# Second block's mixer: three projection blocks split with GpSimd, the convolution's sums in PSUM

## The chip, the cores and the metric

One core of one Trainium2 chip runs the program. The metric is the device time of one execution in microseconds (us). The median of three runs of the kernel before is 1846.14 us (1843.38 to 1847.57).

## What is computed

Two transformer blocks run one after the other on 256 tokens of width 1024, all in float32. The first (two layers, the second with eight experts) is not touched. The second block begins with a mixer, and the change lies there. Cut to what matters:

```python
u = rms_norm(h, mix_norm_g)
q, k, v, glu_a, glu_g = split(u @ w_in)              # 5 x 512 columns
attn_out = moba_attention(q, k, v, rel_bias)         # 8 heads
x = glu_a * sigmoid(glu_g)
x = causal_conv(x, conv_w, 31 taps, per channel) + conv_b
conv_out = silu(layer_norm(x))
h = h + concat(attn_out, conv_out) @ w_out
u = rms_norm(h, ffn_norm_g)
h = h + (silu(u @ w_gate) * (u @ w_up)) @ w_down
```

## The kernel before

**Weights.** All weight matrices come as blocks of 128 x 2048 floats (1 MB). `Stream` (line 52) loads them in a fixed order through SyncE's DMA queue into three raw buffers (`wraw`, `_load`, line 79) and makes two fp32r parts of each (`_split`, line 91): `wh`, a rounded copy made on ScalarE (line 102), and `wl`, the rest, raw minus `wh`, made on VectorE (line 103). A product is then three passes on TensorE, high by high, high by low, low by high (`mm3`). There are three pairs of buffers for the parts, and a fourth during the output products. A raw buffer is free again when `wl` has been made, a pair when the products that read it are done.

A block in `native` is not split: it is multiplied as plain float32 from its raw buffer against an unsplit copy of the input (`xTf`), which TensorE runs as two records for each product (64 for two blocks of 16 products). Its raw buffer is free when these products are done.

**The mixer.** The ten blocks of `w_in_2` are numbered 0 to 9 here: 0 to 3 give gate and value of the four channel tiles of the convolution, 4 and 5 give q, 6 and 7 k, 8 and 9 v. `NATIVE2` says which are native: 0, 1, 4, 5, 6, 7. Blocks 2 and 3, and v's 8 and 9, are split. After each of the blocks 0 to 3 ScalarE makes the sigmoid `ga` (line 1215) and VectorE the product `ug` (line 1216).

`conv(ct)` (line 1226) works on one tile of 128 channels by 256 tokens: ScalarE starts the sum with the last tap and the bias (line 1228), and VectorE adds 30 taps, each one `scalar_tensor_tensor` with a shift of `back` columns, in place in the SBUF tile `cv` (line 1232). The loop behind it issues, for each of four steps, `conv(i)`, the attention scores of two pairs of heads, for the first two steps a block of v, and the values of the step before. Then come the mean over channels (`pmu`, two groups of products on TensorE), the variance (`pvr`), the root on GpSimd, `prs`, SiLU on ScalarE, the split of the result into `oT`, and the output products `Mix.part` into the accumulators `acc0` (PSUM banks 0 and 1, first half of the tokens) and `acc1` (banks 2 and 3). `acc` holds the two halves of 512 output columns in one bank each.

The framework sorts the instructions of each engine by the order in the program and by its estimate of when each is ready, so operations of `conv(1)` can stand between those of `conv(0)`. Each engine then runs its list in order, and waits on semaphores for other engines. Before the change GpSimd has nothing to do from 1535.7 us to 1622.3 us.

Of the kernel before, what the change touches and what calls it, by code (L numbers as in the profile page):

```python
# [10 lines left out]
F32 = mybir.dt.float32  # L11
# [4 lines left out]
AF = mybir.ActivationFunctionType  # L16
ALU = mybir.AluOpType
# [4 lines left out]
T = 256  # L22
# [5 lines left out]
NE = 8  # L28
R_RAW = 3
N_SPLIT = 3  # L30
NATIVE2 = (0, 1, 4, 5, 6, 7)


class Buffers:


    def __init__(self):
        self.pools = []
# [14 lines left out]
class Stream:  # L53

    def __init__(self, tc, raw_pool, pool, blocks, n_raw=R_RAW, n_split=N_SPLIT, native=()):
        self.tc, self.nc = tc, tc.nc
        self.blocks, self.native = blocks, native
        self.raw_bufs, self.split_bufs = Buffers(), Buffers()  # L60
        self.raw_bufs.add(raw_pool, "wraw", n_raw, len(blocks))
        self.split_bufs.add(pool, None, n_split, len(blocks))
        self.ready, self.raws = [], []
        self.n_raw = self.n_used = 0
        self.first = False
        self.limit = len(blocks)
        self.after = ()
        self.load_after = None
        self.before = {}
# [22 lines left out]
    def _split(self, pool):  # L92
        nc = self.nc
        raw = self.raws.pop(0)
        i = self.n_used + len(self.ready)
        wh = pool.tile([P, 2048], F32R, tag="wh", name="wh")
        wl = pool.tile([P, 2048], F32R, tag="wl", name="wl")
        with ExitStack() as queued:
            for ins in self.after:
                queued.enter_context(self.tc.issue_after(ins.ins))  # L100
            for c in self._parts(i):
                nc.scalar.activation(wh[:, c], raw[:, c], AF.Copy)  # L102
                nc.vector.tensor_tensor(wl[:, c], raw[:, c], wh[:, c].bitcast(F32), op=ALU.subtract)  # L103
        self.ready.append((wh, wl))

    def resume(self, after=(), n=None):
# [36 lines left out]
def tile_model(ctx, tc, io, out):  # L143
    nc = tc.nc
    cp = ctx.enter_context(tc.tile_pool(name="cp", bufs=1))
    xp = ctx.enter_context(tc.tile_pool(name="xp", bufs=6))
    rawp = ctx.enter_context(tc.tile_pool(name="rawp", bufs=R_RAW))
    wp = ctx.enter_context(tc.tile_pool(name="wp", bufs=N_SPLIT))
# [3 lines left out]
    def ffn_order(w1, w3, w2, n, lag=1):  # L152
        r = []
        for j in range(n):
            r += [w1[j], w3[j]]
            if j >= lag:
                r.append(w2[j - lag])
        return r + [w2[j] for j in range(n - lag, n)]

    NF, NM = FF // 256, FFE // 512  # L160
    order = [io["w_ab"][i] for i in range(15)] + [io["w_out_ab"][i] for i in range(4)]
# [5 lines left out]
    for i in range(len(steps_) + 1):  # L167
        if i < len(steps_):
            e, j = steps_[i]
            moe_order += [io[n][e][j][kh] for n in ("w1_m", "w3_m") for kh in range(2)]  # L170
        if i:
            e, j = steps_[i - 1]
# [3 lines left out]
    second = len(order)  # L176
    order += [io["w_in2"][i] for i in range(10)] + [io["w_out2"][i] for i in range(4)]
    order += ffn_order(io["w1_2"], io["w3_2"], io["w2_2"], NF)
    ws = Stream(tc, rawp, wp, order, native=[second + i for i in NATIVE2])

    groups = {"acc": (0, 1, 2, 3), "mm": (4, 5, 6, 7), "lg4": (0, 1, 2, 3), "lg": (2, 3), "ppt": (4, 5), "po": (6,),
              "pj": (7,), "acc0": (0, 1), "acc1": (2, 3)}
# [2 lines left out]
    def bank(group, name):  # L185

        i = groups[group][turns[group] % len(groups[group])]
        turns[group] += 1
        return ps.tile([P, 512], F32, tag="bank%d" % i, name=name)
# [19 lines left out]
    def half(nh):  # L209
        return slice(nh * 512, (nh + 1) * 512)  # L210
# [8 lines left out]
    def load_const(pool, name):  # L219
        ap = io[name]  # L220
        t = pool.tile(list(ap.shape), F32, tag=name, name=name, bufs=1)
        load_small(t, ap)
        return t
# [276 lines left out]
    class Mix:  # L500


        def __init__(self, oT, finish):
            self.oT, self.finish = oT, finish
            self.w, self.acc = [], [None, None]
# [49 lines left out]
    with tc.tile_pool(name="l0", bufs=1) as lp:  # L555
# [9 lines left out]
        with tc.tile_pool(name="gla", bufs=1) as gp:  # L565
# [22 lines left out]
            for i in range(2):  # L588
                o = proj_cols(xT)
# [11 lines left out]
            for tt in range(2):  # L601
# [3 lines left out]
                for q in range(2):  # L605
# [5 lines left out]
                    for j in range(2):  # L611
                        rl = g2([P, 2, 256], "rl")
                        nc.scalar.activation(rl[:, :, :S], pis[j][:, :, :S], AF.Relu)
                        for i in range(2):
# [3 lines left out]
                                                           op0=ALU.mult, op1=ALU.add)  # L618
                            first = False
                for r in range(8):  # L620
# [4 lines left out]
                                               op0=ALU.not_equal, op1=ALU.max)  # L625
# [76 lines left out]
            for tt in range(2):  # L702
# [13 lines left out]
                for h in range(4):  # L716
                    nc.vector.scalar_tensor_tensor(o_s[:, h, :], o_s[:, h, :], rs[:, h:h + 1], sg[:, tt, tok(h)],
                                                   op0=ALU.mult, op1=ALU.mult)
# [246 lines left out]
    with tc.tile_pool(name="moer", bufs=4) as mr, tc.tile_pool(name="moe2", bufs=2) as m2:  # L965
# [209 lines left out]
        with tc.high_priority():  # L1175
            for tt in range(2):
# [4 lines left out]
                for nh in range(2):  # L1181
                    c = half(nh)
# [3 lines left out]
                for nh in range(2):  # L1186
                    c = half(nh)
# [9 lines left out]
    with tc.tile_pool(name="s1", bufs=1) as lp:  # L1197
# [3 lines left out]
        cw = load_const(lp, "conv_w")  # L1201
        cpar = load_const(lp, "conv_p")
# [6 lines left out]
        ug = lp.tile([P, 4, T], F32, tag="ug", name="ug")  # L1209
        ga = lp.tile([P, 4, T], F32, tag="ga", name="ga")  # L1210
        cv = lp.tile([P, 4, T], F32, tag="cv", name="cv")
        ws.first = True
        for ct in range(4):
            o = proj_cols(xT, xTf)
# [8 lines left out]
        v = lp.tile([P, 2, 512], F32, tag="v", name="v")  # L1223
        scores, values = attention(t2, t2, qT, kT, v, lambda h: strip[:, h, :], None, oT, 0, on_act=True)

        def conv(ct):

            nc.scalar.activation(cv[:, ct, :], ug[:, ct, :], AF.Identity, bias=cpar[:, 0, ct:ct + 1],
                                 scale=cw[:, ct, 30:31])
            for j in range(30):  # L1230
                back = 30 - j
                nc.vector.scalar_tensor_tensor(cv[:, ct, back:], ug[:, ct, :T - back], cw[:, ct, j:j + 1],  # L1232
                                               cv[:, ct, back:], op0=ALU.mult, op1=ALU.add)

        for i, step in enumerate(STEPS):
            conv(i)
# [5 lines left out]
        with tc.tile_pool(name="t2", bufs=1) as tp, tc.tile_pool(name="t2w", bufs=1) as wo:  # L1242
# [35 lines left out]
            for ct in range(4):  # L1278
                nc.scalar.activation(cv[:, ct, :], cv[:, ct, :], AF.Silu, bias=cpar[:, 2, ct:ct + 1],
                                     scale=cpar[:, 1, ct:ct + 1])  # L1280
# [6 lines left out]
    with tc.tile_pool(name="f2", bufs=2) as fp, tc.tile_pool(name="f2r", bufs=4) as fr, tc.tile_pool(name="f2w", bufs=1) as fw:  # L1287
        fing = bcast(fp, io["fin_g"], "fing")

        o = xp.tile([P, 2, D], F32, tag="b8", name="o")  # L1290
# [149 lines left out]
```

## Time and profile before

| | |
|---|---|
| median of three runs | 1846.14 us |
| the profiled execution: its time / its span | 1845.33 / 1843.5 us |
| TensorE products busy, whole span | 1782.0 us (97%) |
| VectorE busy | 1338.1 us (73%) |
| ScalarE busy | 1096.1 us (59%) |
| GpSimd busy | 83.9 us (5%) |
| mean granted TensorE clock | 0.98 |

In the rows below PE is TensorE, PEld its weight loads, DVE VectorE, ACT ScalarE, POOL GpSimd, SPq SyncE's queue. A row of a timeline gives the start in us from the span's start, the busy time, engine, line, operation, output and inputs, shapes and count; a bracket says how long the engine sat idle before and what ended that. A row that stands for several operations (x14) is a run of them with nothing between. Durations of neighbours on one engine overlap a little, so the step from one start to the next is shorter than the duration. L195 is the line of a helper that issues all products.

### The profile page before, as it was taken

The numbers are of one execution on the slowest core, as the hardware profiler recorded it, in microseconds if no ns is written. First come the engines' busy times: TensorE is split into PE (matmuls) and PEld (weight loads), VectorE is DVE, ScalarE is ACT, GpSimd is POOL, SyncE is SP. The second block draws the span as 40 slices with busy tenths as digits, with TensorE's granted clock in tenths as the row PEclk, the third lists the DMA queues.
The fourth block names the chain that finished last, engine by engine and source line by source line (L and its number), as shares of the span: only waits on it lengthen the run. The fifth ranks groups of instructions, "written<-read, shape, count | busy, mean of one in ns | idle before, by whom it ended". The sixth has DMA issues, their size and how long they took to land. (4 is left out here: it accounts for less than half of the span.)

```text
span 1843.5 us, 24483 instructions
## 1 busy us (share of the span) xinstructions
PE 1782.0 (97%) x9857; PEld 1512.4 (82%) x9857; DVE 1338.1 (73%) x1363; ACT 1096.1 (59%) x1016; POOL 83.9 (5%) x133
## 2 busy tenths in 40 slices
PE   8999999999999999999999999999998987999998
PEld 7887999888778888888788787887886867889997
DVE  6866544545678888888888888888887877955443
ACT  5454433344567777777777777777775754564442
POOL 1101100010010000000000000000002002000000
PEclk9999999999989999999999999999999998999999
DMA  8442985254379999999999999999998933546530
GB/s 297 161 163 103 390 329 186 89 196 158 117 300 423 381 371 371 382 355 366 374 367 368 381 364 375 371 368 373 366 364 321 361 139 140 206 155 250 190 125 24
DMA packets 75418, 512.50 MB, mean 278 GB/s; under 512 B 8572, under 2 KB 8725, under 8 KB 17312
## 3 DMA queue, kind: packets, MB, share of 16 engines
q1 hardware_dynamic: 66096, 475.62, 68.2%
q0 software_dynamic: 8912, 34.70, 5.0%
q8 instruction: 80, 1.31, 0.3%
q10 hardware_dynamic: 288, 0.52, 0.1%
q14 instruction: 42, 0.34, 0.0%
HBM read 495.57 MB, written 19.96 MB: 280 GB/s over the span
## 5 line engine op out<-in xcount | busy, mean ns | idle before, releaser
L103 DVE TENSOR_TENSOR wl<-wraw,wh 128x2048 fp32r<-128x2048 f32 (+1 forms) x446 | 1011.3, 2284 | 306.6 <-ACT wh L102 304.8
L102 ACT ACTIVATE wh<-wraw 128x2048 fp32r<-128x2048 f32 (+1 forms) x446 | 851.8, 1912 | 465.5 <-issue 133.3
L195 PE MATMUL hh<-wl,eTh 128*128 128x512 f32 x896 | 356.0, 397 | 5.2 <-DVE wl L103 5.2
L195 PE MATMUL hh<-wh,eTh 128*128 128x512 f32 x896 | 355.6, 397 | 0.0
L195 PE MATMUL hh<-wh,eTl 128*128 128x512 f32 x896 | 353.5, 395 | 0.0
L195 PE MATMUL pc<-xTh,wh 128*128 128x256 f32 x944 | 270.8, 287 | 1.0 <-ACT xTh L203 1.0
L195 PE MATMUL pc<-xTl,wh 128*128 128x256 f32 x944 | 269.7, 286 | 0.8 <-DVE xTl L204 0.8
L195 PE MATMUL pc<-xTh,wl 128*128 128x256 f32 x944 | 269.6, 286 | 0.0
L195 PEld LDWEIGHTS hh<-wl,eTh 128*128 128x128 f32 x896 | 169.3, 189 | 47.8 <-DVE wl L103 9.5
L195 PEld LDWEIGHTS hh<-wh,eTh 128*128 128x128 f32 x896 | 169.1, 189 | 38.9 <-ACT eTh L203 0.2
L195 PEld LDWEIGHTS hh<-wh,eTl 128*128 128x128 f32 x896 | 169.0, 189 | 38.2
L195 PE MATMUL acc<-wl,mah 128*128 128x512 f32 x448 | 181.7, 406 | 5.9 <-DVE wl L103 5.9
L195 PEld LDWEIGHTS pc<-xTh,wh 128*128 128x128 f32 x944 | 183.2, 194 | 4.0 <-ACT xTh L203 1.4
L195 PEld LDWEIGHTS pc<-xTl,wh 128*128 128x128 f32 x944 | 183.1, 194 | 2.0 <-DVE xTl L204 1.3
L195 PEld LDWEIGHTS pc<-xTh,wl 128*128 128x128 f32 x944 | 183.3, 194 | 0.2 <-issue 0.2
L195 PE MATMUL acc<-wh,mal 128*128 128x512 f32 x448 | 177.6, 397 | 0.3 <-DVE mal L204 0.3
L195 PE MATMUL acc<-wh,mah 128*128 128x512 f32 x448 | 164.2, 396 | 0.5 <-ACT mah L203 0.5
L195 PEld LDWEIGHTS acc<-wl,mah 128*128 128x128 f32 x448 | 85.0, 190 | 24.2 <-DVE wl L103 6.4
L195 PEld LDWEIGHTS acc<-wh,mah 128*128 128x128 f32 x448 | 84.7, 189 | 20.7 <-ACT mah L203 0.9
L195 PEld LDWEIGHTS acc<-wh,mal 128*128 128x128 f32 x448 | 85.2, 190 | 18.5 <-DVE mal L204 0.8
L195 PE MATMUL pt<-wh,xTh 128*128 128x256 f32 x256 | 74.2, 291 | 0.5 <-ACT xTh L203 0.4
L195 PE MATMUL pt<-wl,xTh 128*128 128x256 f32 x256 | 73.6, 288 | 0.2 <-DVE wl L103 0.2
(332 smaller groups left out, 1851.8 us busy)
## 6 DMA issues: line engine op xcount, KB each, us to landing
wraw<-in_w_m_dram SPq DMA_DIRECT2D x336, 1024.0 KB, 7.3
wraw<-in_w_d_dram SPq DMA_DIRECT2D x33, 1024.0 KB, 5.7
wraw<-in_w_dram SPq DMA_DIRECT2D x33, 1024.0 KB, 4.9
wraw<-in_w_ab_dram SPq DMA_DIRECT2D x14, 1024.0 KB, 4.9
wraw<-in_w_cd_dram SPq DMA_DIRECT2D x12, 1024.0 KB, 4.9
wraw<-in_w_in_dram SPq DMA_DIRECT2D x10, 1024.0 KB, 4.9
xg_d<-zero POOLq DMA_DIRECT2D x8, 1024.0 KB, 43.8
rows<-scr POOLq DMA_DIRECT2D x3, 1536.0 KB, 11.6
```

The source lines that it names most:

```text
L102: nc.scalar.activation(wh[:, c], raw[:, c], AF.Copy)
L103: nc.vector.tensor_tensor(wl[:, c], raw[:, c], wh[:, c].bitcast(F32), op=ALU.subtract)
L195: nc.tensor.matmul(o, l, r, start=start, stop=stop, skip_group_check=True)
```

## The change

Block 5 stays native beside 0 and 1; blocks 4, 6 and 7 are now split, their high parts on ScalarE as for all blocks, their low parts on GpSimd. The convolution's running sums move from the SBUF tile `cv` to two PSUM banks, `sums`, tiles 0 and 1 in the first and 2 and 3 in the second, which take the turns of `acc0`. The last tap of each tile writes `cv`; it does not reach column 0, which ScalarE copies.

```diff
--- before.py
+++ after.py
@@ -28,7 +28,8 @@
 NE = 8
 R_RAW = 3
 N_SPLIT = 3
-NATIVE2 = (0, 1, 4, 5, 6, 7)
+NATIVE2 = (0, 1, 5)
+POOL2 = (4, 6, 7)
 
 
 class Buffers:
@@ -54,9 +55,9 @@
 
 
 
-    def __init__(self, tc, raw_pool, pool, blocks, n_raw=R_RAW, n_split=N_SPLIT, native=()):
+    def __init__(self, tc, raw_pool, pool, blocks, n_raw=R_RAW, n_split=N_SPLIT, native=(), on_pool=()):
         self.tc, self.nc = tc, tc.nc
-        self.blocks, self.native = blocks, native
+        self.blocks, self.native, self.on_pool = blocks, native, on_pool
         self.raw_bufs, self.split_bufs = Buffers(), Buffers()
         self.raw_bufs.add(raw_pool, "wraw", n_raw, len(blocks))
         self.split_bufs.add(pool, None, n_split, len(blocks))
@@ -100,7 +101,8 @@
                 queued.enter_context(self.tc.issue_after(ins.ins))
             for c in self._parts(i):
                 nc.scalar.activation(wh[:, c], raw[:, c], AF.Copy)
-                nc.vector.tensor_tensor(wl[:, c], raw[:, c], wh[:, c].bitcast(F32), op=ALU.subtract)
+                engine = nc.gpsimd if i in self.on_pool else nc.vector
+                engine.tensor_tensor(wl[:, c], raw[:, c], wh[:, c].bitcast(F32), op=ALU.subtract)
         self.ready.append((wh, wl))
 
     def resume(self, after=(), n=None):
@@ -176,7 +178,8 @@
     second = len(order)
     order += [io["w_in2"][i] for i in range(10)] + [io["w_out2"][i] for i in range(4)]
     order += ffn_order(io["w1_2"], io["w3_2"], io["w2_2"], NF)
-    ws = Stream(tc, rawp, wp, order, native=[second + i for i in NATIVE2])
+    ws = Stream(tc, rawp, wp, order, native=[second + i for i in NATIVE2],
+                on_pool=[second + i for i in POOL2])
 
     groups = {"acc": (0, 1, 2, 3), "mm": (4, 5, 6, 7), "lg4": (0, 1, 2, 3), "lg": (2, 3), "ppt": (4, 5), "po": (6,),
               "pj": (7,), "acc0": (0, 1), "acc1": (2, 3)}
@@ -1223,14 +1226,19 @@
         v = lp.tile([P, 2, 512], F32, tag="v", name="v")
         scores, values = attention(t2, t2, qT, kT, v, lambda h: strip[:, h, :], None, oT, 0, on_act=True)
 
+        sums = [bank("acc0", "cv") for _ in range(2)]
+
         def conv(ct):
 
-            nc.scalar.activation(cv[:, ct, :], ug[:, ct, :], AF.Identity, bias=cpar[:, 0, ct:ct + 1],
-                                 scale=cw[:, ct, 30:31])
+
+            o = sums[ct // 2][:, ct % 2 * T:(ct % 2 + 1) * T]
+            nc.scalar.activation(o, ug[:, ct, :], AF.Identity, bias=cpar[:, 0, ct:ct + 1], scale=cw[:, ct, 30:31])
             for j in range(30):
                 back = 30 - j
-                nc.vector.scalar_tensor_tensor(cv[:, ct, back:], ug[:, ct, :T - back], cw[:, ct, j:j + 1],
-                                               cv[:, ct, back:], op0=ALU.mult, op1=ALU.add)
+                last = j == 29
+                nc.vector.scalar_tensor_tensor((cv[:, ct] if last else o)[:, back:], ug[:, ct, :T - back], cw[:, ct, j:j + 1],
+                                               o[:, back:], op0=ALU.mult, op1=ALU.add)
+            nc.scalar.activation(cv[:, ct, 0:1], o[:, 0:1], AF.Copy)
 
         for i, step in enumerate(STEPS):
             conv(i)
```

## Rows read from the trace of the kernel before

**Rows 1.** Busy time by stage: start and end, length, engines, granted clock, DMA.
```profile
1545.20:1616.10 70.90, 67.89 (x418) 60.21 (x418) 69.34 (x176) 32.96 (x66) 0.00 (x0) 0.98 0.53 186
1616.10:1644.80 28.70, 28.43 (x160) 22.57 (x159) 14.97 (x23) 19.18 (x37) 1.84 (x5) 1.00 0.23 84
```
**Rows 2.** Timeline of VectorE, the convolution's taps.
```profile
1545.24 2.92 DVE L1232 SCALAR_TENSOR_TENSOR cv<-ug,conv_w,cv 128x226 f32<-128x226 f32 x6 [0.67 <-ACT cv L1228]
...
1550.61 5.41 DVE L1232 SCALAR_TENSOR_TENSOR cv<-ug,conv_w,cv 128x232 f32<-128x232 f32 x14
...
1561.90 20.97 DVE L1232 SCALAR_TENSOR_TENSOR cv<-ug,conv_w,cv 128x247 f32<-128x247 f32 x55
...
1606.50 3.04 DVE L1232 SCALAR_TENSOR_TENSOR cv<-ug,conv_w,cv 128x247 f32<-128x247 f32 x6
...
1615.08 0.48 DVE L1232 SCALAR_TENSOR_TENSOR cv<-ug,conv_w,cv 128x255 f32<-128x255 f32 x1
```
**Rows 3.** Groups by line: count, busy us, mean ns, idle; wl 1545-1615.5, wh 1505-1650.
```profile
L103 DVE TENSOR_TENSOR wl<-wraw,wh 128x2048 fp32r<-128x2048 f32 x7 | 15.9, 2282 | 0.9 <-ACT wh L102 0.9
...
L102 ACT ACTIVATE wh<-wraw 128x2048 fp32r<-128x2048 f32 x13 | 24.8, 1911 | 14.4 <-DMA wraw<-in_w_in_dram 8.8 <-PE acc L195 3.4 <-PE pt L195 1.3
```
**Rows 4.** Timeline of TensorE, the projection blocks.
```profile
1534.70 14.58 PE L195 MATMUL pc<-xTf,wraw 128*128 128x256 f32 x64
1548.92 0.47 PE L195 MATMUL pc<-xTh,wh 128*128 128x256 f32 x1
...
1560.62 27.79 PE L195 MATMUL pc<-xTf,wraw 128*128 128x256 f32 x128
1588.34 0.72 PE L195 MATMUL lg<-kT,qT 64*128 64x128 f32 x8
```
**Rows 5.** Timeline of all engines around the end of block 2.
```profile
1551.86 0.28 PE L195 MATMUL pc<-xTh,wl 128*128 128x256 f32 x1
...
1554.74 0.28 PE L195 MATMUL pc<-xTh,wl 128*128 128x256 f32 x1
...
1555.06 0.39 ACT L1215 ACTIVATE ga<-pc 128x256 f32<-128x256 f32 x1 [3.73 <-PE pc L195]
...
1555.93 0.41 DVE L1216 TENSOR_TENSOR ug<-ga,pc 128x256 f32<-128x256 f32 x1
...
1556.27 1.22 DVE L1232 SCALAR_TENSOR_TENSOR cv<-ug,conv_w,cv 128x240 f32<-128x240 f32 x3
...
1556.38 0.60 ACT L1228 ACTIVATE cv<-ug,conv_p,conv_w 128x256 f32<-128x256 f32 x1 [0.94 <-DVE ug L1216]
```
**Rows 6.** Timeline of GpSimd and VectorE in the first block, around 75 us.
```profile
75.08 3.97 POOL L646 TENSOR_TENSOR sg<-sg,gnorm 128x1024 f32<-128x1024 f32 x1 [26.65 <-ACT sg L644]
...
74.54 2.29 DVE L103 TENSOR_TENSOR wl<-wraw,wh 128x2048 fp32r<-128x2048 f32 x1 [3.46 <-ACT wh L102]
77.91 1.28 DVE L668 TENSOR_TENSOR QK<-E,kaT 128x128 f32<-128x128 f32 x1 [1.08 <-ACT E L663]
...
79.32 0.28 DVE L668 TENSOR_TENSOR QK<-E,kaT 128x128 f32<-128x128 f32 x1
```
**Rows 7.** Issues by line: count, KB each, median us from issue to landing.
```profile
wraw<-in_w_in_dram SPq DMA_DIRECT2D x10, 1024.0 KB, 4.9
```
**Rows 8.** Groups of VectorE by line, inputs in PSUM (po) and in SBUF (cv).
```profile
L204 DVE TENSOR_TENSOR oTl<-po,oTh 128x256 fp32r<-128x256 f32 x4 | 1.7, 417 | 2.4 <-ACT oTh L203 2.3
...
L204 DVE TENSOR_TENSOR oTl<-cv,oTh 128x256 fp32r<-128x256 f32 x4 | 1.5, 418 | 0.0
```
**Rows 9.** Timelines of ScalarE, TensorE and VectorE from 1612 to 1636 us.
```profile
1617.99 1.06 ACT L1261 ACTIVATE ga<-cv 128x1024 f32<-128x1024 f32 x1 [0.74 <-DVE cv L1260]
...
1612.21 0.58 PE L195 MATMUL acc<-wh,oTh 128*128 128x512 f32 x1
...
1620.16 1.84 PE L195 MATMUL pvr<-c,ga 128*128 128x1 f32 x16
...
1634.50 0.62 PE L195 MATMUL acc<-wh,oTl 128*128 128x512 f32 x2
...
1633.82 1.09 DVE L204 TENSOR_TENSOR oTl<-cv,oTh 128x256 fp32r<-128x256 f32 x3
```
**Rows 10.** Timeline of TensorE, the stall ahead of v's second block.
```profile
1600.51 0.77 PE L481 MATMUL ppt<-ident,z 128*128 128x128 f32 x2 [1.27 <-ACT z L470]
```

## Prediction

> **What bounds the kernel now.** The page comes first: TensorE is busy almost throughout, but that is a mean over stages, so I go to the stage that the change edits, the second block's mixer, from the first projection product at 1534.70 us to the last output product at about 1644.8. The table by stage cuts it at the end of the convolution [rows 1]. In the 70.90 us up to 1616.10 VectorE is busy 69.34 and TensorE 67.89; in the 28.70 us behind it TensorE is busy 28.43 and VectorE 14.97. So two engines take turns: VectorE sets when the convolution ends, TensorE fills the rest. What VectorE does in that first stretch is read from its timeline and its groups [rows 2, 3]: the convolution is 120 operations of L1232 (4 channel tiles by 30 taps), between them 7 low parts wl at 2.28 us, and the softmax pieces. The first tap starts at 1545.24 and the last ends at 1615.47. Nothing in the change makes the start earlier: the first two blocks, on which it waits, stay native.
>
> **Part 1: three blocks leave plain float32.** Four native blocks stand back to back from 1560.62 to 1588.34, 27.72 us, so 6.93 each; the two split ones before them fill 1548.92 to 1560.62, 5.85 each [rows 4]. Each of blocks 4, 6, 7 saves 1.08 us on TensorE, 3.2 us in all: the projections would end at 1585.1.
>
> **Part 2: their high and low parts.** ScalarE gets three more high parts at 1.91 us [rows 3]. They fall between 1549 and 1567, where ScalarE sits idle between gates (3.73 us before the one at 1555.06 [rows 5]), so I cost them at nothing; if that cover were gone, 5.7 us of ScalarE stand ahead of the gates. GpSimd makes the low parts. Its price is in the first block: a 128x1024 product of two SBUF tensors lasts 3.97 us from 75.08, but it starts under a VectorE low part that began at 74.54 and ends at 76.83. Counted from there to 79.05 it is 2.22 us, so 4.4 for 2048 (an estimate from this row; 7.9 if all of the 3.97 were its own) [rows 6]. Then by block: a load lands in 4.9 us [rows 7], the high part takes 1.9, the low part 4.4 to 7.9. Block 4's raw buffer comes free at about 1541.8, when block 0's products end (half of the 14.2 us of [rows 4]), so its low part is there by 1553 to 1557, wanted at 1560.6. Block 6 loads behind block 3's low part (1550.4): ready by 1562 to 1565.1 plus any sharing of the transfer, wanted at 1573.4. Block 7 loads into the buffer that GpSimd's own subtract releases: ready by 1566 to 1573, wanted at 1579.2. Even the slow ends leave 3 us. SyncE's queue is passed in order: the loads of blocks 7, 8, 9 now wait for GpSimd's subtracts instead of products that end 10 us later, so a late subtract would hold all later loads; on time, it brings them forward. GpSimd's next work is the root after the variance, at 1622, long after.
>
> That same place shows the price of GpSimd and VectorE reading SBUF together: an L668 of two SBUF tensors, normally 0.28 us, took 1.28, ending with GpSimd's 79.05 [rows 6]. [...] The low parts wl still have two; by my times none of them meets a GpSimd subtract (block 3's runs 1548 to 1550.4, block 8's after 1570), so I add nothing, and up to 4.4 us for each that does.
>
> **Part 3: the sums in PSUM.** Removed is nothing; 120 taps remain, the last of each tile writing SBUF, and four one-column copies come on ScalarE. What a tap costs when it reads and writes PSUM no row shows. The nearest: the low part of an attention output read from PSUM lasts 417 ns, that of a convolution output read from SBUF 418 [rows 8]. Reading PSUM costs nothing; writing is not shown. Ends: below, the 0.34 us step of a plain 256-column operation against 0.38 of a tap, if PSUM shed the difference, −4.8 us over 120; above, +0.11 us each, what a tap alone pays (next paragraph), +13 us. I take 0, by the reading rows.
>
> [...]
>
> **The order it forces.** A tap on the sum just written starts 0.49 us after the one before it (six from 1545.24); with two tiles interleaved the step is 0.38 (55 from 1561.90), and near the end, one tile left, 0.52 [rows 2]. So interleaving is worth 0.11 us a tap. Before, tiles 0 and 1 interleave from 1550.7 on. After, they share a bank. Does that part them? The gate at 1555.06 reads only the first half of block 2's bank, written by product 24 at 1551.86; ScalarE was idle, yet it started only after product 48 at 1554.74 [rows 5]. The program orders two engines by whole bank. Tile 1's start on ScalarE therefore waits for all of tile 0's taps and its column copy; tile 3's for tile 2's. Tile 0 pairs with tile 2 instead, whose start ends at 1556.98 [rows 5].
> - 1545.24 to 1556.98: 11.7 us, less one wl (2.2) and two gate products (0.34 each [rows 5]), is 18 taps at 0.49; before, 6 + 14 + 2 = 22. Four taps late, 4 x 0.38 = **1.5 us**.
> - Two handovers (last tap, copy, start 0.6 us, first tap): about 1.2 us each with a lone tile, 3 taps at 0.11: **0.6 us**.
> - Ahead of the mean: tile 3's copy on ScalarE, **0.4 us** (2.3 if a high part stands before it).
>
> Queued behind tile 1's start on ScalarE are copies of q and k and high parts; TensorE has four banks for projections, so a wait of a few us there reaches nobody. Last, the sums hold banks 0 and 1 until tile 3's copy, and the first output product (1612.21 now [rows 9]) goes to these banks: those for the second half of the columns must wait until about 1618. TensorE fills its lead with them no more.
>
> **The sum.** The convolution ends 2.5 us later. Behind it the path is mean, square, variance, SiLU, splits, products. It is tight: the splits end at 1634.9 and a product of the second convolution tile starts at 1634.50 [rows 9]. What the earlier TensorE can return there is its queue before the variance: the square ends at 1619.05, the 16 products start at 1620.16 [rows 9], 1.1 us. The other 2.1 us of its 3.2 turn into waiting. Net +2.5 − 1.1 = +1.4 us. The profiled execution took 1845.33 us (span 1843.5, 1.8 around it), 0.8 under the median of the three runs: **1846.7 us**.
>
> **The rivals.**
> - The lead reaches the end. For it: TensorE is busy 28.43 of the last 28.70 us, so work done earlier counts if it is output products that are ready. Against it: the banks held, the tight splits. All of it: 1845.3 − 3.2 = 1842.1; if the stall at 1600.51 (1.27 us [rows 10]) goes too, 1840.8.
> - Taps get cheaper in PSUM: −4.8 + 1.4 gives 1841.9, with the lead 1840. Nothing shows it.
> - **Slower: a tap costs more in PSUM.** One mechanism: VectorE is full from 1545 to 1616, so x ns a tap delay the convolution's end by 0.12x us, and all behind it. It decides from about 20 ns (2.4 + 1.4 = 3.8 us). At 60 ns, about half the lone tile's surcharge: 1853.9. For it: the write is unseen. Against: the reads cost nothing.
> - GpSimd does not do it beside the others: its subtracts hold VectorE's two-input operations or come late, up to 3 x 4.4 us: 1858. Against: the times above, 3 us or more in hand.
>
> **How the numbers follow.** Forecast 0.52 (alone 1844 to 1849); the lead reaches the end 0.13; cheaper taps 0.07; dearer taps 0.20; GpSimd in the way 0.08. About 0.2%, 3.7 us, is what a measurement can tell from no change. Faster by more: half of the second case and the third, 0.13. Within: the first and the other half, 0.59. Slower: the last two, 0.28. The range 1841 to 1856 leaves out the fastest part of the third case and GpSimd in the way, some 0.15.
>
> **What would show it.** Projections end near 1585 (if not, GpSimd was late: a wait for wl on TensorE). GpSimd's subtract lasts near 4.4 us and no tap beside it is longer. Taps keep steps of 0.38 and 0.49; tile 1's start on ScalarE stands behind tile 0's last tap. The convolution ends near 1618, and TensorE waits before the first products of banks 0 and 1. I am wrong if tiles 0 and 1 still interleave, if a tap's step moves by over 20 ns, or if the last stretch shortens by over 2 us.

## The result, and the profile after

Both kernels ran eleven times. The changed one took 1857.11 us in the median (1852.56 to 1861.96), the one before 1846.39 (1842.67 to 1851.88); the ratio is 1.0066, with a 95% interval from 1.0050 to 1.0082. So the change costs 12 us, 0.7%. The prediction was 1846.7, no change; its range ended at 1856. Every ratio here and below leaves out executions in the chip's slower state; there was one, of e8 below, at 2492.74 us.

The profiled execution after took 1852.56 us (span 1850.8), 7.2 us more than that of before (1845.33, span 1843.5). That understates the loss: its first projection product starts at 1528.52, against 1534.70 before, though nothing ahead of the mixer is changed; TensorE's granted clock in the first 100 us was 1.00 in the one execution and 0.95 in the other. All times below are therefore taken from the first projection product. From there to the end it is 308.8 us before and 322.3 after: 13.5 us lost.

By stage (start and end, length, busy us of TensorE, its weight loads, VectorE, ScalarE, GpSimd; granted clock, DMA share, GB/s), from the first tap to the last, and from there to the end:

```profile
1538.67:1624.29 85.62, 79.60 (x533) 69.24 (x531) 72.57 (x182) 44.15 (x86) 13.82 (x3) 0.94 0.45 160
1624.29:1850.80 226.51, 209.93 (x1422) 193.88 (x1422) 107.44 (x85) 87.81 (x86) 6.14 (x15) 0.97 0.40 147
```

The first line answers [rows 1]: what took 70.3 us (1545.24 to 1615.56) with VectorE busy 68.8 takes 85.6 with VectorE busy 72.6. The convolution ends 95.8 us after the first product, against 80.9. Of these 14.9 us, 3.8 are more busy time on VectorE: the taps take 2.6 us more (50.5 for 47.9), and 1.1 is softmax work and attention outputs that used to stand behind the last tap. The rest is waiting. Where it waits stands in its timeline (answers [rows 2]):

```profile
1538.67 2.44 DVE L1239 SCALAR_TENSOR_TENSOR cv<-ug,conv_w,cv 128x226 f32<-128x226 f32 x5 [0.64 <-ACT cv L1235]
...
1556.44 0.42 DVE L1219 TENSOR_TENSOR ug<-ga,pc 128x256 f32<-128x256 f32 x1 [0.96 <-ACT ga L1218]
1556.78 4.64 DVE L1239 SCALAR_TENSOR_TENSOR cv<-ug,conv_w,cv 128x250 f32<-128x250 f32 x12
1563.72 2.29 DVE L105 TENSOR_TENSOR wl<-wraw,wh 128x2048 fp32r<-128x2048 f32 x1 [2.31 <-ACT wh L103]
1565.93 9.04 DVE L1239 SCALAR_TENSOR_TENSOR cv<-ug,conv_w,cv 128x226 f32<-128x226 f32 x24
...
1598.76 2.29 DVE L105 TENSOR_TENSOR wl<-wraw,wh 128x2048 fp32r<-128x2048 f32 x1 [2.20 <-ACT wh L103]
...
1607.14 0.42 DVE L464 CUSTOM_DVE_ANT_0 z<-lg,strip 128x256 f32<-128x256 f32 x1 [1.77 <-PE lg L198]
...
1615.91 3.04 DVE L1239 SCALAR_TENSOR_TENSOR cv<-ug,conv_w,cv 128x243 f32<-128x243 f32 x6
1620.37 0.42 DVE L207 TENSOR_TENSOR oTl<-po,oTh 128x256 fp32r<-128x256 f32 x1 [1.42 <-ACT oTh L206]
1620.71 3.58 DVE L1239 SCALAR_TENSOR_TENSOR cv<-ug,conv_w,cv 128x249 f32<-128x249 f32 x7
```

Two things are to be seen. A tap costs what it did (24 in 9.04 us with two tiles; 5, 6 and 7 of a lone tile at 0.49 to 0.51). And VectorE waits in front of work that is not taps: a gate product, a low part, a score, a softmax sum, an attention output, 11.8 us in all (waits of over 0.15 us) where it was 0.9. At the low parts and the score, taps that could have filled the wait stand behind it in its list. The wait for the score goes round by TensorE: at 1603.15 it has waited 2.01 us for ScalarE's copy of tile 1's column 0, which the first products of the mean read, and these stand ahead of the score in its own list. ScalarE's timeline shows the starts of tiles 1 and 3, each behind the copy of column 0 that ends the other tile of its bank:

```profile
1554.22 1.92 ACT L103 ACTIVATE wh<-wraw 128x2048 fp32r<-128x2048 f32 x1 [2.08 <-PE pc L198]
1556.04 0.37 ACT L1218 ACTIVATE ga<-pc 128x256 f32<-128x256 f32 x1
1561.78 1.91 ACT L103 ACTIVATE wh<-wraw 128x2048 fp32r<-128x2048 f32 x1 [5.38 <-DMA wraw<-in_w_in_dram]
1564.08 0.16 ACT L1241 ACTIVATE cv<-cv 128x1 f32<-128x1 f32 x1
1564.27 0.57 ACT L1235 ACTIVATE cv<-ug,conv_p,conv_w 128x256 f32<-128x256 f32 x1
...
1592.77 0.14 ACT L1241 ACTIVATE cv<-cv 128x1 f32<-128x1 f32 x1
1592.94 0.57 ACT L1235 ACTIVATE cv<-ug,conv_p,conv_w 128x256 f32<-128x256 f32 x1
```

GpSimd and TensorE did what was forecast. Their timelines (answer [rows 6] and [rows 4]) show 4.6 us a low part, and one native block of 32 records, 6.7 us to the next:

```profile
1544.58 4.63 POOL L105 TENSOR_TENSOR wl<-wraw,wh 128x2048 fp32r<-128x2048 f32 x1 [15.05 <-DVE cv L1239]
1552.21 9.19 POOL L105 TENSOR_TENSOR wl<-wraw,wh 128x2048 fp32r<-128x2048 f32 x2 [3.01 <-ACT wh L103]
```
```profile
1559.85 7.07 PE L198 MATMUL pc<-xTf,wraw 128*128 128x256 f32 x32
1566.57 0.47 PE L198 MATMUL pc<-xTh,wh 128*128 128x256 f32 x1
```

Behind the convolution TensorE, which had run ahead, ran out of products. By stage from the subtraction of the mean on:

```profile
1625.29:1630.29 5.00, 4.65 (x28) 3.66 (x26) 1.38 (x2) 3.17 (x3) 0.32 (x2) 1.00 0.00 0
1630.29:1635.29 5.00, 1.19 (x4) 0.93 (x4) 3.12 (x4) 4.26 (x6) 0.59 (x1) 0.60 0.00 0
1635.29:1640.29 5.00, 3.27 (x7) 2.18 (x8) 4.32 (x6) 1.92 (x6) 0.00 (x0) 0.50 0.66 228
```

In the last two slices it is busy 4.5 of 10 us, with the granted clock at 0.60 and 0.50. In the kernel before it is busy 5.00 of 5 in each such slice from 1616.73 to 1636.73, at 1.00; this is the second of them:

```profile
1621.73:1626.73 5.00, 5.00 (x31) 3.82 (x30) 2.25 (x6) 2.33 (x5) 0.91 (x2) 1.00 0.00 0
```

Two of its waits there are for the convolution's own output: 2.82 us for the first high part, 1.66 for the low part. That low part stands behind two weight low parts in VectorE's list:

```profile
1633.79 4.48 DVE L105 TENSOR_TENSOR wl<-wraw,wh 128x2048 fp32r<-128x2048 f32 x2
```

### The profile page after: what moved, and what is told of

It reads as the page before. It is cut to its first block, busy times and chain, and to the rows that moved or that the text cites. A ratio compares the mean times of both kernels' runs of the same rounds, so it can differ in the third digit from the quotient of the medians.

```text
span 1850.8 us, 24596 instructions
## 1 busy us (share of the span) xinstructions
PE 1778.7 (96%) x9905; PEld 1509.4 (82%) x9905; DVE 1339.6 (72%) x1363; ACT 1101.7 (60%) x1023; POOL 95.6 (5%) x136
## 5 line engine op out<-in xcount | busy, mean ns | idle before, releaser
L198 PE MATMUL pc<-xTh,wh 128*128 128x256 f32 x992 | 283.5, 286 | 1.5 <-ACT xTh L206 1.5
L198 PE MATMUL pc<-xTl,wh 128*128 128x256 f32 x992 | 282.1, 284 | 0.8 <-DVE xTl L207 0.8
L198 PE MATMUL pc<-xTh,wl 128*128 128x256 f32 x992 | 282.0, 284 | 0.0
L198 PEld LDWEIGHTS pc<-xTh,wh 128*128 128x128 f32 x992 | 191.4, 193 | 4.5 <-ACT xTh L206 1.9
L198 PEld LDWEIGHTS pc<-xTl,wh 128*128 128x128 f32 x992 | 191.3, 193 | 1.8 <-DVE xTl L207 1.1
L198 PEld LDWEIGHTS pc<-xTh,wl 128*128 128x128 f32 x992 | 191.4, 193 | 0.1
```

The costliest lines, as they stand in the source:

```text
L198: nc.tensor.matmul(o, l, r, start=start, stop=stop, skip_group_check=True)
```

## The experiments

Each kernel ran beside the kernel before on the same chip. The table gives the ratio with its 95% interval, and from the one profiled execution of each: the end of the last tap and the start of the subtraction of the mean, in us after the first projection product; VectorE's idle time between first and last tap, in waits of over 0.15 us; and what follows from the subtraction to the end.

| kernel | ratio | last tap ends | idle | subtraction | to the end |
|---|---|---|---|---|---|
| before | 1 | 80.9 | 0.9 | 82.0 | 226.8 |
| after | 1.0066 [1.0050, 1.0082] | 95.8 | 11.8 | 96.8 | 225.5 |
| e1 sums in PSUM alone | 1.0073 [1.0044, 1.0103] | 93.3 | 8.5 | 94.6 | 225.5 |
| e2 GpSimd alone | 1.0068 [1.0046, 1.0090] | 98.8 | 4.1 | 101.1 | 221.2 |
| e3 banks by parity | 1.0023 [1.0005, 1.0040] | 90.6 | 9.6 | 93.4 | 221.3 |
| e4 two tiles in PSUM | 1.0020 [1.0004, 1.0035] | 90.2 | 8.2 | 92.3 | 224.5 |
| e5 PSUM alone, parity | 1.0047 [1.0025, 1.0069] | 90.0 | 8.1 | 91.3 | 226.8 |
| e6 split on VectorE | 1.0045 [1.0024, 1.0066] | 89.2 | 1.1 | 90.4 | 225.0 |
| e7 parity, column from ug | 1.0030 [1.0009, 1.0051] | 88.2 | 6.8 | 90.5 | 221.0 |
| e8 as e7, five on GpSimd | 1.0004 [0.9992, 1.0015] | 88.4 | 10.1 | 90.9 | 220.9 |
| e9 as e5, VectorE's old order | 1.0051 [1.0038, 1.0065] | 86.9 | 7.8 | 89.6 | 228.6 |
| e10 as e7, VectorE's old order | 1.0056 [1.0042, 1.0070] | 91.8 | 11.7 | 94.8 | 226.6 |
| e11 before, VectorE in e5's order | 1.0035 [1.0020, 1.0049] | 88.3 | 6.4 | 90.7 | 226.7 |
| e12 PSUM, two old lists | 1.0018 [1.0004, 1.0031] | 85.6 | 5.4 | 87.0 | 226.6 |
| e13 as e12, with GpSimd | 1.0012 [0.9998, 1.0027] | 85.9 | 6.7 | 87.3 | 228.2 |
| e14 as e8, taps first | 1.0008 [0.9995, 1.0021] | 83.6 | 7.0 | 91.0 | 221.0 |

**The two halves apart, and the bank.** e1 keeps the native set of before; what is left of the change is the sums in PSUM:

```diff
-NATIVE2 = (0, 1, 5)
-POOL2 = (4, 6, 7)
+NATIVE2 = (0, 1, 4, 5, 6, 7)
+POOL2 = ()
```


> Blocks 4, 6, 7 are native again and GpSimd idle; only the sums stay in PSUM. I count from the first projection product to the end of the span: 308.8 us before, 322.3 after. Bank order (tile 1 may start only when tile 0's sum is whole, tile 3 only behind tile 2, so that one tile is left alone at the end): nearly all of the loss is here too, 320 to 325, and VectorE still works on the last tile alone for some 25 taps. GpSimd and its loads (high parts that stand waiting ahead of a tile's start on ScalarE): without them the loss goes, 308 to 311.

It loses as much as the whole change. So GpSimd is not needed for the loss. e2 is the other half: the three splits on GpSimd, the taps in SBUF as before.

```diff
-            o = sums[ct // 2][:, ct % 2 * T:(ct % 2 + 1) * T]
-            nc.scalar.activation(o, ug[:, ct, :], AF.Identity, bias=cpar[:, 0, ct:ct + 1], scale=cw[:, ct, 30:31])
...
+            nc.scalar.activation(cv[:, ct, :], ug[:, ct, :], AF.Identity, bias=cpar[:, 0, ct:ct + 1],
+                                 scale=cw[:, ct, 30:31])
...
```


> The three blocks are split with GpSimd as after the change; the sums are back in the SBUF tile cv. Same stretch, 308.8 before, 322.3 after. Bank order: that loss is gone, but each tap has two SBUF inputs now, and if GpSimd and VectorE exclude each other for a whole instruction, three subtracts hold a tap each for 4 to 4.6 us: 13 us of VectorE, of which TensorE's 3.2 us return at most some, 316 to 322, with three taps of 2 to 5 us in the trace. If they don't exclude each other: 306 to 309. GpSimd and its loads as the cause: 320 or more without any long tap.

It loses as much again, by another mechanism. VectorE's and GpSimd's timelines:

```profile
1547.97 5.32 DVE L1235 SCALAR_TENSOR_TENSOR cv<-ug,conv_w,cv 128x232 f32<-128x232 f32 x2
...
1565.30 0.40 DVE L1219 TENSOR_TENSOR ug<-ga,pc 128x256 f32<-128x256 f32 x1
1565.63 13.75 DVE L1235 SCALAR_TENSOR_TENSOR cv<-ug,conv_w,cv 128x250 f32<-128x250 f32 x14
```
```profile
1547.39 5.14 POOL L105 TENSOR_TENSOR wl<-wraw,wh 128x2048 fp32r<-128x2048 f32 x1 [14.63 <-ACT wh L103]
1561.06 8.70 POOL L105 TENSOR_TENSOR wl<-wraw,wh 128x2048 fp32r<-128x2048 f32 x1 [8.53 <-ACT wh L103]
1569.72 4.77 POOL L105 TENSOR_TENSOR wl<-wraw,wh 128x2048 fp32r<-128x2048 f32 x1
```

Beside GpSimd's subtracts 2 taps take 5.32 us and 14 take 13.75; at the 0.38 of [rows 2] they would take 0.8 and 5.3. The difference, 13 us, is VectorE held, in three taps alone, one for each subtract (4.82, 4.40 and 4.79 us, from 1547.97, 1565.63 and 1569.95); no other lasts over 0.49. GpSimd is held too: its second subtract takes 8.70 us instead of 4.6, while the taps from 1561 to 1565 keep their step. That subtract ends 4.5 us after the start of the gate product of 1565.30, which reads PSUM; that GpSimd got its turn only there is the author's guess, no run tried it apart. In the kernel after, with the sums in PSUM, no tap lasts over 0.49 us. The expectation's first case had a tap held under each of three subtracts, 13 us of VectorE; the trace agrees.

e3 and e4 take the whole change and part neighbouring tiles: e3 gives tiles 0 and 2 one bank, 1 and 3 the other; e4 gives tiles 0 and 1 a bank each and leaves 2 and 3 in SBUF.

```diff
-            o = sums[ct // 2][:, ct % 2 * T:(ct % 2 + 1) * T]
+            o = sums[ct % 2][:, ct // 2 * T:(ct // 2 + 1) * T]
```


> As after the change, but tiles 0 and 2 share one bank and 1 and 3 the other, so neighbours in the program may interleave. Bank order: tiles 0 and 1 interleave, then 2 and 3; the convolution ends near where it did before, 308 to 312 from the first projection product (308.8 before, 322.3 after). GpSimd and its loads: 318 to 324, since nothing of them is changed.

```diff
-            o = sums[ct // 2][:, ct % 2 * T:(ct % 2 + 1) * T]
+            o = sums[ct][:, :T] if ct < 2 else cv[:, ct]
...
-            nc.scalar.activation(cv[:, ct, 0:1], o[:, 0:1], AF.Copy)
+            if ct < 2:
+                nc.scalar.activation(cv[:, ct, 0:1], o[:, 0:1], AF.Copy)
```


> Tiles 0 and 1 sum in PSUM, each in its own bank; tiles 2 and 3 in SBUF as before the change, since their taps come after GpSimd's three subtracts (over at 1561.4 after the change). Bank order: no two tiles share a bank, 306 to 310 (308.8 before, 322.3 after), and no tap longer than 0.5 us unless tile 2 starts before GpSimd is done. GpSimd and its loads: 318 to 324.

Both come back by about 0.45%, 8 us: e3 differs from after in the banks of tiles 1 and 2 alone, and the intervals lie apart. Tiles that share a bank and want to run together are the larger part of the loss. But neither comes back as far as expected: from the first product to the end they take 314.7 and 316.7 us, where at most 312 and 310 were forecast, and both end the convolution near 90, not 81, with VectorE idle 8 to 10 us. Something else costs.

**What else: the split, the copy, or VectorE's low parts?** e5 joins e1 and e3 (the sums in PSUM alone, parity banks). e6 has the three splits with VectorE making the low parts, taps in SBUF (POOL2 empty in e2). e7 is e3 with column 0 made from `ug`, and e8 is e7 with v's two low parts on GpSimd too:

```diff
+            nc.scalar.activation(cv[:, ct, 0:1], ug[:, ct, 0:1], AF.Identity, bias=cpar[:, 0, ct:ct + 1], scale=cw[:, ct, 30:31])
...
-            nc.scalar.activation(cv[:, ct, 0:1], o[:, 0:1], AF.Copy)
...
-POOL2 = (4, 6, 7)
+POOL2 = (4, 6, 7, 8, 9)
```


> The sums in PSUM with the two tiles of a bank two places apart (0 and 2, 1 and 3), the three blocks multiplied natively as before, nothing on GpSimd. The sums in PSUM with neighbouring tiles in a bank, also without GpSimd, ended the convolution 93.3 us after the first projection product (before: 80.9) and were at 1.0073 of before. Theory A (the whole of that loss was the bank): the end comes back to 81 to 84 us, VectorE's idle time in the convolution under 3 us, the time within 0.2% of before. Theory B (something else of the sums in PSUM also costs, such as ScalarE's copy of column 0, or the order that the planner makes of it): the end stays at 87 us or later, and the time 0.2% to 0.4% over before. If A holds, what the run with both changes and the parity banks still loses (end at 90.6) belongs to the blocks that are split.

> The three blocks are split, but VectorE makes their low parts, 2.28 us each, and the sums stay in SBUF: neither GpSimd nor PSUM. TensorE gains 3 x 1.1 = 3.2 us, VectorE has 6.8 us more work in a stretch in which it is busy 69 of 70 us. Theory A (VectorE's work decides the end): the end of the convolution goes from 80.9 to about 88 us after the first product and the time 5 to 7 us over before (1.003 to 1.004). Theory B (the splits that come earlier also make ScalarE and VectorE stand behind loads): VectorE's idle time in the convolution rises from 1 to 4 us or more, the end is at 91 or later, the time 8 us or more over before. Theory C (TensorE's lead decides): the time is equal to before or under it.

> The changed kernel with the parity banks, and column 0 of cv made by ScalarE directly from ug at the tile's start, so that nothing of ScalarE reads the sum's bank after the taps. Theory A (the copy of column 0 holds the next user of the bank, and ScalarE with it): the end of the convolution goes from 90.6 (with the copy) to 87 us or earlier, VectorE's idle time from 9.6 to under 6 us, time 1.000 to 1.001 of before. Theory B (the copy costs nothing; what is left is VectorE waiting for its own split of the next block, which stands behind a load): 90 to 91 us and 1.002, as with the copy.

> As the run before (parity banks, column 0 from ug), and GpSimd also makes the low parts of the two value blocks, which VectorE made: VectorE loses 2 x 2.28 us of work and no longer stands behind the loads of these two blocks. Theory A (VectorE's own split of the next block, placed ahead of taps and waiting for ScalarE's high part and its load, is the second cause): the end of the convolution comes 5 us or more earlier than in the run before, VectorE's idle time falls by 2 us or more, and the time is at or below that of before (0.997 to 1.000). Theory B (the waits are for TensorE's projections and the attention, and only move): the end comes at most 2 us earlier and the time is 1.002.

e5 falls on the side of its theory B: without GpSimd, and with neighbours parted, the end is still at 90.0. (Its time is not told apart from e1's: the intervals overlap.) e6 is its theory A: VectorE is busy 77.0 us for 68.8, and hardly idle (1.1); the work decides there. e7 ends the taps 2.4 us earlier than e3 but its time is not told apart from e3's; no verdict. e8 is at the time of before, with the end where its theory B has it (88.4) and VectorE more idle (10.1) than in e3, e5 and e7: less work on it did not end the waits.

What e5 shows is where VectorE waits:

```profile
1556.74 17.47 DVE L1239 SCALAR_TENSOR_TENSOR cv<-ug,conv_w,cv 128x245 f32<-128x245 f32 x45
1576.51 2.29 DVE L105 TENSOR_TENSOR wl<-wraw,wh 128x2048 fp32r<-128x2048 f32 x1 [2.31 <-ACT wh L103]
...
1604.95 2.29 DVE L105 TENSOR_TENSOR wl<-wraw,wh 128x2048 fp32r<-128x2048 f32 x1 [2.18 <-ACT wh L103]
```

The 45 taps ahead of the first value block's low part are 55 in the kernel before [rows 2], and there VectorE does not wait for it:

```profile
1582.80 2.27 DVE L103 TENSOR_TENSOR wl<-wraw,wh 128x2048 fp32r<-128x2048 f32 x1
```

Counted over the whole list of VectorE, as the framework sorted it when the program was built, these taps stand ahead of:

```
                       first value block's low part   first score
before                             89                     101
e1 (PSUM alone)                    73                      84
e5 (PSUM alone, parity)            75                      86
after                              43                      73
```

Most of the way from 89 to 43 comes with the splits: with the three blocks split and the sums in SBUF, e6 has 63 and e2 52.

Between the gates of two tiles the list of before has 14 taps, that of e5 12 and 13: with the sums in PSUM the framework sets fewer taps in the same stretch, though a tap runs no slower (45 in 17.47 us in e5). Why it does was not tried. VectorE stood where the list puts it: 2.31 us at the low part of 1576.51, with 11 taps next in the list, run from 1578.72 on.

**Is it the list?** e11 is the kernel before with nothing but an order imposed: VectorE's 165 instructions of the stretch as they stand in e5. e9 is the reverse, e5 with VectorE's order of before; e10 the same on e7. The numbers in the list are places in program order:

```diff
+        dve = [i for i in nc.cur_bb.bb.instructions[since:] if i.engine == mybir.EngineType.DVE]
+        for earlier, later in zip(DVE_TURNS, DVE_TURNS[1:]):
+            tc.add_manual_dep(dve[later], dve[earlier].name, mybir.DependencyInfo(mybir.DependencyClass.NoSync, mybir.DependencyReason.DATA), reason="order")
```


> The kernel before, nothing changed but VectorE's order: its 165 instructions of the stretch in the order that the planner made for sums in PSUM (75 taps ahead of the first value block's low part, 86 ahead of the first score); sums in SBUF, blocks native. Theory A (the order alone is the second cause): the convolution ends at 87 to 90 us in place of 80.9, VectorE is idle 6 to 8 us in it, and the time is 1.003 to 1.005 of before, as with the sums in PSUM. Theory B (it needs PSUM): end under 84 us, time within 0.2% of before.

> The sums in PSUM, banks by parity, blocks native, no GpSimd (the run that ended the convolution at 90.0 us and was at 1.0047), with VectorE's 165 instructions of the stretch put in the order that they have in the kernel before: there the planner set 89 taps ahead of the first value block's low part and 101 ahead of the first score, here 75 and 86. Theory A (the planner counts a tap in PSUM as longer, so sets fewer taps between its other work, and VectorE stands at that work and finishes the taps late): the end comes back to 81 to 84 us, VectorE's idle time in the convolution goes from 8.1 to under 3 us, and the time is 0.999 to 1.001 of before. Theory B (something that PSUM does at run time, such as the starts and copies by ScalarE): the end stays at 87 us or later and the time at 1.003 or more.

> The whole change with banks by parity and column 0 from ug (the run that ended at 88.2 us and was at 1.0030), with VectorE's instructions in the order of the kernel before. If the order is the second cause, the end is at 80 to 83 us, and TensorE's 3 x 1.1 us that GpSimd's low parts save are left on TensorE: the time is at or below before, 0.998 to 1.000 (0 to 4 us gained). If GpSimd's low parts or their loads cost something else, the time stays at 1.002 or more.

e11 meets its theory A in each number: end at 88.3, idle 6.4 us, 1.0035. Its timeline has e5's waits, with the sums in SBUF:

```profile
1563.24 17.49 DVE L1245 SCALAR_TENSOR_TENSOR cv<-ug,conv_w,cv 128x245 f32<-128x245 f32 x45
1582.96 2.29 DVE L115 TENSOR_TENSOR wl<-wraw,wh 128x2048 fp32r<-128x2048 f32 x1 [2.24 <-ACT wh L114]
...
1611.57 2.29 DVE L115 TENSOR_TENSOR wl<-wraw,wh 128x2048 fp32r<-128x2048 f32 x1 [1.82 <-ACT wh L114]
```

So the order alone costs 0.35%, 6.5 us. The other engines' lists came out nearly as before: TensorE's is the same for 75 us, ScalarE's up to the end of the convolution but for one exponential that follows a later score. e9 and e10 missed: 1.0051 and 1.0056, e9 close to its theory B. Holding one engine's list made the framework sort the others anew around it. In e9 the second value block's products stand on TensorE ahead of the first transposes of softmax weights (`ppt`), where two pairs of these came first, and on ScalarE two high parts stand ahead of the first exponential, which begins at 1597.60; VectorE waits 2.83 us for it at 1598.51. In e10 VectorE waits 3.90 us at 1577.81 for a tile's start on ScalarE. Two things were changed, so e9 says nothing on PSUM. e12 therefore holds ScalarE's list too (the starts of tiles 2 and 3 behind the query evictions, column 0 from `ug`), which leaves TensorE's list as it was up to the products of the mean, 81 us after the first; e13 adds the GpSimd half.

```diff
+        for queue, placed in ((mybir.EngineType.DVE, DVE_TURNS), (mybir.EngineType.Activation, ACT_TURNS)):
+            own = [i for i in nc.cur_bb.bb.instructions[since:] if i.engine == queue]
```


> Sums in PSUM (banks by parity, column 0 from ug), blocks native, no GpSimd; VectorE's 165 and ScalarE's 61 instructions of the stretch in the order of the kernel before (but for the starts of tiles 2 and 3, which wait for a bank and stand behind the first and the second query eviction); TensorE's list up to the end of the convolution comes out as before. Theory A (order is all that is left): the end of the convolution is 81 to 83 us after the first product (before 80.9; the two starts that wait for a bank cost about 0.5 us each, as they did with VectorE alone ordered), VectorE idle 1 to 3 us, the time 0.999 to 1.001 of before. Theory B (PSUM costs at run time): the end at 86 us or later and the time 1.003 to 1.005, as with VectorE alone ordered.

> As the run before, with the change's other half: blocks 4, 6 and 7 split, their low parts made by GpSimd; ScalarE's three more high parts stand where the planner puts them. If order is all, the convolution ends at 80 to 83 us and TensorE's 3 x 1.1 us reach the end in full or in part: 0.998 to 1.000 of before. If the three splits cost something of their own, such as ScalarE's 3 x 1.9 us ahead of the gates or VectorE standing 1.4 us for the gate that is late, the end is at 84 us or later and the time 1.001 to 1.003.

e12 is at 1.0018, 0.29% below e5. That agrees with e11, but it is at the edge of the noise (the intervals overlap), and e12 also makes column 0 from `ug`. It stops short of its theory A (85.6, idle 5.4). What is left is partly seen. The two starts that wait for a bank cost VectorE 0.31 and 0.32 us. And the first block of `w_out` is loaded 54.5 us after the first product, where it was 50.4: its raw buffer is the one that block 7's products release, not the one that the low part at 1580.59 releases. ScalarE waits for that load, VectorE for ScalarE. From e12's timelines of SyncE's queue, ScalarE and VectorE:

```profile
1585.80 9.49 SPq L105 DMA_DIRECT2D wraw<-in_w_out_dram  x4
```
```profile
1590.70 1.91 ACT L122 ACTIVATE wh<-wraw 128x2048 fp32r<-128x2048 f32 x1 [4.29 <-DMA wraw<-in_w_out_dram]
```
```profile
1573.18 7.50 DVE L1260 SCALAR_TENSOR_TENSOR cv<-ug,conv_w,cv 128x226 f32<-128x226 f32 x20 [0.32 <-ACT cv L1255]
...
1592.64 2.29 DVE L124 TENSOR_TENSOR wl<-wraw,wh 128x2048 fp32r<-128x2048 f32 x1 [2.12 <-ACT wh L122]
```

Which buffer a load gets is the framework's choice as well; that it makes the whole of the remaining 0.18% was not tried. A further wait, 2.63 us ahead of the fourth output block's low part (0.93 before), was not followed. e13 is not told apart from e12 or from before: with the old lists the GpSimd half gains nothing that can be measured.

**Does the taps' end decide?** e14 holds the lists of e8 on all three engines and moves only taps in VectorE's: 6 more ahead of the first score, 5 more ahead of the second `w_out` block's low part, and that of the fourth block later (it is the one that the expectation calls the third).

> The run with five low parts on GpSimd, banks by parity and column 0 from ug (time 1.0004 of before, convolution ending 88.4 us after the first product, VectorE idle 10.1 us in it), with the lists of ScalarE and TensorE kept as they were and VectorE's list changed alone: 6 taps more ahead of the first score (where it waited 2.19 us), 5 more ahead of the low part of the second output block (2.03 us), and that of the third output block later (2.71 us). Theory A (the taps' end is what the block's tail waits for): the end comes to 82 to 84 us, VectorE's idle time to 3 to 5 us, and the time to 0.997 to 0.999 of before. Theory B (scores and values are then as late as the taps, so that the tail waits for those): VectorE's idle time only moves to its waits for scores and for the attention's outputs, the end stays at 86 us or later and the time at 1.000.

The taps end at 83.6, 4.7 us earlier than in e8, as theory A has it, and the time does not move (1.0008), as theory B has it. VectorE's idle time only falls to 7.0; at the last gate it now waits 3.20 us, in e8 1.24. The end of e8's and of e14's convolution on VectorE:

```profile
1621.86 0.42 DVE L207 TENSOR_TENSOR oTl<-po,oTh 128x256 fp32r<-128x256 f32 x1 [1.38 <-ACT oTh L206]
1623.00 1.22 DVE L1268 TENSOR_TENSOR cv<-cv,pmu 128x1024 f32<-128x1024 f32 x1 [0.72 <-PE pmu L198]
```
```profile
1619.81 0.42 DVE L249 TENSOR_TENSOR oTl<-po,oTh 128x256 fp32r<-128x256 f32 x1 [4.31 <-ACT oTh L248]
1620.15 1.21 DVE L1311 TENSOR_TENSOR cv<-cv,pmu 128x1024 f32<-128x1024 f32 x1
```

The subtraction of the mean stands behind the last attention output in VectorE's list, and that comes 89.7 and 90.7 us after the first product; the subtraction starts at 90.9 and 91.0. In the kernel before, it starts at 82.0, ahead of the last two attention outputs (1623.80 and 1628.71):

```profile
1616.73 1.22 DVE L1260 TENSOR_TENSOR cv<-cv,pmu 128x1024 f32<-128x1024 f32 x1 [0.42 <-PE pmu L195]
```

The wait was moved, not removed. No version was found that beats the kernel before.

## Why the prediction was wrong

**What held.** A tap in PSUM costs nothing more: 24 with two tiles in 9.04 us, 0.38 each, as in [rows 2]. The rival with dearer taps falls, though its 1853.9 lies near the measured time. GpSimd takes 4.6 us a low part (estimate 4.4), is done at 1561.40, and holds no tap: the sum put nothing on taps beside its subtracts, which no row of before shows, and in after no tap lasts over 0.49 us. So the rival "GpSimd in the way" falls too, whose 1858 lies nearest to the measured time; e1 loses as much without GpSimd. The projections end sooner, as forecast: the last of them ends 49.9 us after the first product begins, before 53.7; 0.4 of these 3.8 us lies in the first two blocks, which are unchanged. (The second key eviction starts only 2.0 us earlier, at 51.7: ScalarE makes a high part ahead of it.) Tiles 0 and 1 do not interleave, because the program orders ScalarE's start by whole bank: tile 1's, at 1564.27, follows tile 0's copy at 1564.08. (The last tap of the kernel before ends at 1615.56, not 1615.47; no sum goes by it.)

**The term that was mis-sized: the order by bank.** It was priced at four late taps and two handovers, 2.1 us with the tail's 0.4 beside. After against e3, the same kernel with neighbours in one bank and parted, makes it 1.0066 against 1.0023, 8 us. (Without GpSimd, e1 against e5, the times are not told apart, 1.0073 and 1.0047; e1 ends the taps 3.3 us later.) As VectorE's own work the price was about right: the taps take 2.6 us more than before, in e3 1.0 more. What was missed is the waiting. The working counted tile 3's start as a handover like tile 1's. It stands behind tile 2's copy at 1592.77, when the list already alternates taps with scores, so tile 3 is alone from 1602 on, for 26 taps, and ends late. Of the 7.6 us between the two profiles, from the first product on, 3.4 lie ahead of the subtraction and 4.2 behind it, where TensorE runs out of products (below).

**The step that failed: taking the lists as they were.** The sum assumed VectorE's order of before, with the same waits around it. It kept VectorE's low parts, scores and outputs where they stood, and let a wait of ScalarE reach "nobody". The change rewrote the lists: 43 taps instead of 89 ahead of the first value block's low part, 73 instead of 101 ahead of the first score. VectorE then waits at low parts and a score (2.31, 2.20, 1.77 us) with taps ready behind them. e11 shows that this mechanism costs: e5's order (75 and 86 taps) on the kernel before, nothing else in the program changed, costs 0.35%. What the list of after itself costs, apart from the bank, no run gives; e3, parted, still loses 0.23%, 4 us. No rival held this.

**ScalarE's cover was thinner than costed.** The three high parts were put at nothing. The one at 1554.22 waits for a pair of buffers until TensorE has done with it, and the gate behind it is late: VectorE stands 0.96 us at 1556.44. In e13 that is 1.43 and 1.55 us at two gates.

**Where TensorE's lead went.** The forecast gave 1.1 of 3.2 us back and let the rest turn to waiting. From the subtraction to the end it is 225.5 us for 226.8, so 1.3 came back; and the waiting is there, 5.5 us of 10, at a granted clock of 0.60 and 0.50. In e2, e3, e7, e8 and e14 the same stretch takes 221, some 5.8 us less than before; in e3 and e8 TensorE does not run dry (busy 4.29 of 5 us at the worst in the 20 us behind the subtraction). That fits the rival "the lead reaches the end", and is not shown to be it: the subtraction is late in all five, so TensorE has done more ahead of it. The convolution's late end takes more than that gives. The 4.2 us between after and e3 in that stretch are TensorE's waits: 1.41, 2.82 and 1.66 us in after, for the root, the first high part and the low part of the convolution's output; 0.71 and 0.33 in e3. One cause is again the list: ahead of that low part VectorE has two weight low parts in after (4.48 us), one in e3 (2.29). Why e3 still has products to do in the meantime was not followed.

## What to carry to other kernels

Moving a buffer to another memory, or an operation to another engine, can also change the order in which a sorting framework sets everything else on these engines; compare the instruction lists of the two programs, count what stands ahead of each wait, and only then sum durations. Two sums that should run at the same time belong in different PSUM banks where, as here, the program lets a start on another engine wait for the whole bank: after against e3, 1.0066 against 1.0023, makes that 8 us. And when a wait is taken away, name the next instruction in the same list: the subtraction behind the last attention output made 4.7 us worth nothing.

## What the runs showed of the hardware

In the kernel after, scalar-tensor-tensor operations on sums in PSUM, read and written, keep the step that they have in SBUF in the kernel before: 0.38 us a tap of 226 to 255 columns with two tiles interleaved (24 in 9.04 us; 55 in 20.97 before), 0.51 with one tile left (7 in 3.58; 6 in 3.04 before). In e2, with the sums in SBUF, taps and GpSimd's subtracts, which each read two SBUF tensors, held each other up: one tap beside each of three subtracts takes 4.4 to 4.8 us, where no other lasts over 0.49, and the subtracts take 5.1, 8.7 and 4.8 us, where those of the kernel after take 4.6. In the kernel after, behind a stretch in which TensorE was busy 1.19 of 5 us at a granted clock of 0.60, the clock was at 0.50 in the next five, while it worked 3.27 of them.
